# Two query heads turned by one transpose, and low weight parts subtracted on GpSimd, in a hybrid S5 and attention encoder layer

## The chip, the core and the metric

The kernel runs on one core of one Trainium2 chip. The metric is the device time of one execution in microseconds; the time before is a median of 3 runs. The profile comes from one further execution.

## What is computed

The layer works on two sequences of 512 tokens with 1024 features, in fp32. The part that the change touches, cut from the reference:

```
h = rms_norm(x, ln1)
q, k, v, u, g_att, g_ssm = split(h @ w_in)                # 16 query heads, 4 key-value heads of 64
q = rms_norm(q.reshape(b, s, 16, 64), q_gain)             # per head
k = rms_norm(k.reshape(b, s, 4, 64), k_gain)
y_att = windowed_attention(q, k, v, sink, bias, mask)     # blocks of 128 queries, 3 key blocks, a sink per head
y_ssm = s5_branch(u, ...)                                 # y * sigmoid(y @ w_glu + b_glu)
mixed = sigmoid(g_att) * y_att + sigmoid(g_ssm) * y_ssm
x = x + mixed @ w_out
y = x + square(relu(rms_norm(x, ln2) @ w_up)) @ w_down
```

## The kernel before

Each fp32 product is made of three products of reduced-precision operands. An operand is split into a high part (ScalarE copies it to the type fp32r, which rounds it) and a low part (the operand minus the high part); `mm3` multiplies high by high, high by low and low by high. A weight that streams in is thus loaded by SP into a raw tile, copied by ScalarE (L683, L730) and subtracted by VectorE (L684, L731).

The attention stage is a loop of eight passes, one for each key-value head `j` and sequence `sq` (`steps`), and each pass has four steps, one for each block `qb` of 128 queries. The order of the instructions on TensorE, ScalarE, VectorE and GpSimd is the order of the code; SP's order is set by a scheduler. A step interleaves three things:

- The current unit: scores of the four heads (L823), bias and maximum (`largest`, L827), exponentials (L833).
- The unit before: its probabilities are transposed (L839), split into `ph` (ScalarE, L843) and `pl` (VectorE, L848) and multiplied by the values (L855). It has three key blocks when its query block is 1 or 2, so in steps with `qb` 2 and 3, and two otherwise.
- A query tile of the next pass, class `Tile`: 24 matmuls (L772), the square (L778), its sum (L782), the power on GpSimd (L784, L785), the norm `qn` (L789). One step later `turn` transposes the four heads of the tile (L794) into PSUM, `high` (L799) scales them by the gain into rows 0 to 63 of `queries`, `low` (L802) makes the low part in rows 64 to 127. The keys lie in both halves of the rows, so that one score matmul adds the products of both parts.

`pieces_of` gives a pass its weight pieces: the query weights of the next head (`weight_pieces`: four pieces in pass 0, then two in each of passes 1 to 4), and the GLU weights (`glu_pieces`: two pieces in pass 6, four in pass 7). Pass 5 has none. A piece is loaded and copied at the end of a step, and its subtraction is returned as `lower`, which the next step calls behind its third maximum; the last one is called behind the loop. The raw tiles have two buffers (`c_raw`), so a load waits for the subtraction of the piece two before it.

The denominators of the softmax (`Divide`) are inverted and transposed in step 1 of the next pass, written by SP to `rs_scr` (L883), read back spread over the rows as `fac` (L888), and multiplied into the output at the head of step 3 (`multiply`, L893), behind `largest(0)`. GpSimd also issues DMAs: one copy of `y_scr` per step of passes 1 to 4 (L982), and the gates' loads (`load_gates`, L693).

The 128-row tile `gain_q` holds the gain twice, in rows 0 to 63 and in rows 64 to 127.

Of the kernel before, what the change touches and what calls it, by code (L numbers as in the profile page):

```python
# [12 lines left out]
F32 = mybir.dt.float32  # L13
F32R = mybir.dt.float32r
I32 = mybir.dt.int32
AF = mybir.ActivationFunctionType
ALU = mybir.AluOpType
AX = mybir.AxisListType

P = 128  # L20
# [7 lines left out]
CB = 256  # L28
N_HEADS = 16
N_KV = 4  # L30
G = 4
# [32 lines left out]
def hybrid_layer(ctx, tc, x, rel, onehot, w_qkv, w_ug, vectors, lam, coefs, w_glu, w_out, ln2,  # L64
                 w_up, w_down, out):
    nc = tc.nc
    V, S, PE, GP, SP = nc.vector, nc.scalar, nc.tensor, nc.gpsimd, nc.sync
# [36 lines left out]
    ident = const.tile([P, P], F32, name="ident")  # L104
# [5 lines left out]
    bglu_sb, gain_q, gain_k, nsink = [vec[:, a:b] for a, b in ((0, 8), (8, 9), (9, 10), (10, 26))]  # L110
# [561 lines left out]
    wq = wq_cm.__enter__()  # L672
    glu_w, glu_ps, glu_in = {}, {}, {}

    def glu_pieces(m, pool):

        def piece(i):
            if i == 0:
                glu_w[m] = [pool.tile([P, KT, P], F32R, tag=tag, name="g" + tag) for tag in ("c_hi", "c_lo")]
            hi, lo = [q[:, i * KT // 2:(i + 1) * KT // 2, :] for q in glu_w[m]]  # L680
            raw = cpool.tile([P, KT // 2, P], F32, tag="c_raw", name="c_raw")
            SP.dma_start(raw, w_glu[m][:, i * KT // 2:(i + 1) * KT // 2, :])
            S.copy(hi, raw)  # L683
            return lambda: V.tensor_sub(lo, raw, hi.bitcast(F32))  # L684

        return [lambda i=i: piece(i) for i in range(2)]

# [7 lines left out]
    with tc.tile_pool(name="att", bufs=2, reuse_waits="tile") as ap, tc.tile_pool(name="attc", bufs=1, reuse_waits="tile") as ac:  # L695
# [20 lines left out]
        def weight_pieces(j):  # L716

            weights[j] = []
            pool = wq if j % 2 == 0 else cpool

            def piece(i):

                if i % 2 == 0:
                    weights[j].append((pool.tile([P, KT // 2, CB], F32R, tag="c_hi", name="w_hi"),
                                       pool.tile([P, KT // 2, CB], F32R, tag="c_lo", name="w_lo")))
                hi, lo = weights[j][-1]
                sl = slice(i % 2 * 2, i % 2 * 2 + 2)
                raw = cpool.tile([P, 2, CB], F32, tag="c_raw", name="w_raw")
                SP.dma_start(raw, w_qkv[Q_BLK + j][:, i * 2:i * 2 + 2, :])
                S.copy(hi[:, sl, :], raw)  # L730
                return lambda: V.tensor_sub(lo[:, sl, :], raw, hi[:, sl, :].bitcast(F32))  # L731

            return [lambda i=i: piece(i) for i in range(4)]

# [24 lines left out]
        class Tile:  # L759
# [30 lines left out]

            def turn(self):
                self.pt = self.pt or acc()
                for h in range(G):
                    PE.transpose(self.pt[0:64, h * P:(h + 1) * P], self.qn[:, h], ident)  # L794

            def high(self):
                self.ptv = self.pt[0:64].rearrange("p (h t) -> p h t", h=G)
                self.dst = queries[self.key][:, :, self.t * P:(self.t + 1) * P]
                S.activation(self.dst[0:64], self.ptv, AF.Copy, scale=gain_q[0:64])  # L799

            def low(self):
                V.scalar_tensor_tensor(self.dst[64:128], self.ptv, gain_q[0:64], self.dst[0:64].bitcast(F32),  # L802
                                       op0=ALU.mult, op1=ALU.subtract)

        class Unit:

# [151 lines left out]
        def pieces_of(i):  # L958

            if i == 0:  # L960
                return weight_pieces(1)
            if i == 6:
                return glu_pieces(0, wq)
            if i == 7:
                return glu_pieces(1, cpool) + glu_pieces(2, cpool)
            if i % 2 == 1:
                pending[:] = weight_pieces(i // 2 + 2) if i // 2 + 2 < N_KV else []
                return pending[:2]
            return pending[2:]
# [580 lines left out]
```

## Time and profile before

| | us |
|---|---|
| median of 3 runs | 1511.8 (1508.45 to 1513.73) |
| the profiled execution | 1509.57 |
| its span | 1507.8 |
| TensorE matmul, busy | 1452.1 |
| TensorE weight load, busy | 1232.2 |
| VectorE, busy | 1116.3 |
| ScalarE, busy | 763.4 |
| GpSimd, busy | 192.4 |

The attention loop lies between 460 and 695 us of the span. In a row of the timeline the columns are start, duration, engine, line, operation, tiles (out<-in), shapes and count; behind them, in brackets, stands the idle time of the engine and what ended it. In a row of the groups by shape, the figures behind the first bar are the busy time and the mean ns of one instruction, then the idle time ahead of them. In a row of one line's instructions the three durations are minimum, median and maximum in ns. PE is TensorE, PEld its weight loads, DVE VectorE, ACT ScalarE, POOL GpSimd, SP the engine that issues most DMAs (SPq its queue).

### The profile page before, as it was taken

How to read it: one execution, taken by the hardware profiler on the slowest of the kernel's cores; microseconds unless marked ns; L12 is line 12 of the kernel's file. 1: busy time of each engine (PE TensorE's matmuls, PEld its weight loads, DVE VectorE, ACT ScalarE, POOL GpSimd, SP SyncE). 2: the span in 40 equal slices, each digit the busy share in tenths (PEclk: the TensorE clock that was granted, in tenths of full speed). 3: DMA queues.
4: the chain of work that ended last, by engine and by line, in shares of the span. 5: the costliest groups of instructions: out<-in, count | busy, mean ns of one | idle time of the engine just before them, and what ended most of it. 6: DMA issues, size and time to landing. Idle time of an engine off the chain costs nothing. (4 is left out here: it accounts for less than half of the span.)

```text
span 1507.8 us, 22144 instructions
## 1 busy us (share of the span) xinstructions
PE 1452.1 (96%) x8074; PEld 1232.2 (82%) x8074; DVE 1116.3 (74%) x2015; ACT 763.4 (51%) x1362; POOL 192.4 (13%) x362
## 2 busy tenths in 40 slices
PE   6999999999999999997999989999999999999998
PEld 4788888888999998985787878888888888888787
DVE  7998859986647998886985478777777588575653
ACT  6777852235436787783343255544555443433332
POOL 3143341002232332220100000000000000000000
PEclk9999999999999999998999999999999999999999
DMA  4454469239731444373644234444443694454431
GB/s 173 140 168 168 164 211 344 98 111 352 279 103 36 149 138 142 111 257 110 224 164 170 94 103 173 154 153 154 154 154 126 251 361 135 154 181 154 126 122 61
DMA packets 102141, 249.69 MB, mean 166 GB/s; under 512 B 12266, under 2 KB 23786, under 8 KB 102032
## 3 DMA queue, kind: packets, MB, share of 16 engines
q1 hardware_dynamic: 58352, 135.88, 27.6%
q0 software_dynamic: 18048, 57.72, 11.1%
q10 hardware_dynamic: 25632, 54.67, 9.7%
q8 instruction: 64, 1.05, 0.3%
q14 instruction: 45, 0.37, 0.1%
HBM read 173.74 MB, written 90.21 MB: 175 GB/s over the span
## 5 line engine op out<-in xcount | busy, mean ns | idle before, releaser
L185 PE MATMUL acc<-act,c_hi 128*128 128x512 f32 x768 | 249.8, 400 | 1.0 <-DVE act L304 1.0
L117 PE MATMUL bank<-b_lo,a_hi 128*128 128x512 f32 x448 | 174.6, 390 | 1.3 <-DVE b_lo L1419 1.1
L118 PE MATMUL bank<-b_hi,a_lo 128*128 128x512 f32 x448 | 174.3, 389 | 0.0
L116 PE MATMUL bank<-b_hi,a_hi 128*128 128x512 f32 x448 | 173.5, 389 | 0.0
L185 PEld LDWEIGHTS acc<-act,c_hi 128*128 128x128 f32 x768 | 142.2, 189 | 29.2 <-DVE act L304 2.4
L185 PE MATMUL acc<-act,c_lo 128*128 128x512 f32 x384 | 152.5, 397 | 0.0
L1418 ACT CAST a_hi<-d_a 128x1024 fp32r<-128x1024 f32 x56 | 59.1, 1054 | 179.5 <-PE bank L117 176.1
L116 PE MATMUL bank<-act,act 128*128 128x512 f32 x368 | 144.3, 392 | 4.9 <-ACT act L1308 4.9
L117 PE MATMUL bank<-act,act 128*128 128x512 f32 x368 | 144.0, 391 | 0.0
L118 PE MATMUL bank<-act,act 128*128 128x512 f32 x368 | 143.9, 391 | 0.0
L1419 DVE TENSOR_TENSOR a_lo<-d_a,a_hi 128x1024 fp32r<-128x1024 f32 x56 | 68.5, 1223 | 100.0 <-ACT a_hi L1418 100.0
L772 PE MATMUL acc<-w_hi,act 128*128 128x256 f32 x512 | 116.1, 295 | 0.0
L117 PEld LDWEIGHTS bank<-b_lo,a_hi 128*128 128x128 f32 x448 | 84.1, 188 | 19.6 <-DVE b_lo L1419 2.3
L116 PEld LDWEIGHTS bank<-b_hi,a_hi 128*128 128x128 f32 x448 | 84.1, 188 | 17.6
L118 PEld LDWEIGHTS bank<-b_hi,a_lo 128*128 128x128 f32 x448 | 84.1, 188 | 17.4
L123 PE MATMUL acc<-act,gc_hi 128*128 128x512 f32 x256 | 83.9, 407 | 13.7 <-ACT ga L1133 10.7
L772 PEld LDWEIGHTS acc<-w_hi,act 128*128 128x128 f32 x512 | 86.9, 189 | 3.7
L116 PEld LDWEIGHTS bank<-act,act 128*128 128x128 f32 x368 | 69.6, 189 | 19.8 <-ACT act L1308 5.3
L185 PEld LDWEIGHTS acc<-act,c_lo 128*128 128x128 f32 x384 | 72.6, 189 | 13.8 <-DVE c_lo L176 0.5
L833 ACT ACTIVATE p<-p,nmx 128x257 f32<-128x257 f32 (+1 forms) x128 | 72.2, 564 | 22.7 <-DVE nmx L827 21.1
L118 PEld LDWEIGHTS bank<-act,act 128*128 128x128 f32 x368 | 69.6, 189 | 14.8 <-DVE act L1309 0.4
L117 PEld LDWEIGHTS bank<-act,act 128*128 128x128 f32 x368 | 69.6, 189 | 14.4
(328 smaller groups left out, 3426.5 us busy)
## 6 DMA issues: line engine op xcount, KB each, us to landing
d_a<-a_scr SPq DMA_DIRECT2D x56, 512.0 KB, 3.6
u_raw<-in_w_up_dram SPq DMA_DIRECT2D x32, 512.0 KB, 5.1
a_scr<-t ACTq DMA_DIRECT2D x64, 256.0 KB, 5.0
k<-in_w_down_dram SPq DMA_DIRECT2D x32, 512.0 KB, 6.0
c_raw<-in_w_ug_dram SPq DMA_DIRECT2D x48, 256.0 KB, 3.8
a_scr<-a ACTq DMA_DIRECT2D x46, 256.0 KB, 2.1
ct_scr<-ctab POOLq DMA_DIRECT2D x16, 576.0 KB, 3.9
ctab_in<-ct_scr POOLq DMA_DIRECT2D x16, 576.0 KB, 7.8
```

The source lines that it names most:

```text
L116: PE.matmul(ps, a[0], b[0], start=first, stop=False)
L117: PE.matmul(ps, a[0], b[1], start=False, stop=False)
L118: PE.matmul(ps, a[1], b[0], start=False, stop=last)
L123: PE.matmul(ps, w[wi][:, k, :], rows[yi], start=k + p == 0, stop=k == KT - 1 and p == 2)
L185: PE.matmul(ps, w[wi][:, k, :], hT[s][hi][:, k, :], start=n == 0, stop=n == 3 * KT - 1)
L772: PE.matmul(self.ps, hT[sq][act][:, k, col:col + P], w[:, k % 4, :], start=i == 0, stop=i == 3 * KT - 1)
L833: S.activation(p, p, AF.Exp, bias=self.nmx[:, h:h + 1], scale=-1.0, accum_out=self.sums[:, h, self.qb:self.qb + 1])
L1418: S.copy(hi, src)
L1419: V.tensor_sub(lo, src, hi.bitcast(F32))
```

## The change

`turn` transposes two heads at once: the 128 columns of two neighbouring heads become 128 rows of PSUM, so a tile takes two transposes in place of four. The even heads then lie in rows 0 to 63 and the odd ones in rows 64 to 127. `high` and `low` become two instructions each, one for the even and one for the odd heads, on 64 rows by 256 columns in place of 64 by 512. For odd heads the high part stands in rows 64 to 127 of `queries` and the low part in rows 0 to 63.

The subtraction of the query weight pieces, and of the GLU pieces that are taken inside the loop, moves from VectorE to GpSimd (18 subtractions). The GLU pieces behind the loop stay on VectorE.

```diff
-    def glu_pieces(m, pool):
+    def glu_pieces(m, pool, eng=V):
...
-            return lambda: V.tensor_sub(lo, raw, hi.bitcast(F32))
+            return lambda: eng.tensor_tensor(lo, raw, hi.bitcast(F32), op=ALU.subtract)
...
-                return lambda: V.tensor_sub(lo[:, sl, :], raw, hi[:, sl, :].bitcast(F32))
+                return lambda: GP.tensor_tensor(lo[:, sl, :], raw, hi[:, sl, :].bitcast(F32), op=ALU.subtract)
...
             def turn(self):
                 self.pt = self.pt or acc()
-                for h in range(G):
-                    PE.transpose(self.pt[0:64, h * P:(h + 1) * P], self.qn[:, h], ident)
+                for m in range(2):
+                    PE.transpose(self.pt[:, m * P:(m + 1) * P],
+                                 self.qn[:, 2 * m:2 * m + 2].rearrange("p e d -> p (e d)"), ident)
 
             def high(self):
-                self.ptv = self.pt[0:64].rearrange("p (h t) -> p h t", h=G)
-                self.dst = queries[self.key][:, :, self.t * P:(self.t + 1) * P]
-                S.activation(self.dst[0:64], self.ptv, AF.Copy, scale=gain_q[0:64])
+                self.ptv = self.pt[:, 0:CB].rearrange("p (m t) -> p m t", m=2)
+                self.dst = [queries[self.key][:, e::2, self.t * P:(self.t + 1) * P] for e in range(2)]
+                for dst, rows in zip(self.dst, (slice(0, 64), slice(64, 128))):
+                    S.activation(dst[rows], self.ptv[rows], AF.Copy, scale=gain_q[rows])
 
             def low(self):
-                V.scalar_tensor_tensor(self.dst[64:128], self.ptv, gain_q[0:64], self.dst[0:64].bitcast(F32),
-                                       op0=ALU.mult, op1=ALU.subtract)
+                for dst, rows, other in zip(self.dst, (slice(0, 64), slice(64, 128)), (slice(64, 128), slice(0, 64))):
+                    V.scalar_tensor_tensor(dst[other], self.ptv[rows], gain_q[rows], dst[rows].bitcast(F32),
+                                           op0=ALU.mult, op1=ALU.subtract)
...
-                return glu_pieces(0, wq)
+                return glu_pieces(0, wq, GP)
...
-                return glu_pieces(1, cpool) + glu_pieces(2, cpool)
+                return glu_pieces(1, cpool, GP) + glu_pieces(2, cpool, GP)
```

Three places show how the instructions move. The lines of the changed kernel are 3 higher from here on (L805 is `low`, L830 the maximum, L851 the low part of the probabilities, L818 the copy of the sink). On VectorE, in step 1 of pass 2, from the reciprocal of the denominators to the low part of the queries, before:

```order
L875 RECIPROCAL rsum<-sm 128x16
L827 ISA p,nmx<-sps,bias,vec 128x384
L827 ISA nmx 128x1
L731 TENSOR_TENSOR w_lo<-w_raw,w_hi 128x512
L848 TENSOR_TENSOR pl<-tps,ph 128x512
L827 ISA p,nmx<-sps,bias,vec 128x384
L827 ISA nmx 128x1
L802 SCALAR_TENSOR_TENSOR qa<-acc,vec,qa 64x4x128
```

The same stretch of the changed kernel:

```order
L878 RECIPROCAL rsum<-sm 128x16
L830 ISA p,nmx<-sps,bias,vec 128x384
L830 ISA nmx 128x1
L851 TENSOR_TENSOR pl<-tps,ph 128x512
L830 ISA p,nmx<-sps,bias,vec 128x384
L830 ISA nmx 128x1
L805 SCALAR_TENSOR_TENSOR qa<-acc,vec,qa 64x2x128 x2
```

The subtraction is gone from between the maximum and the low part of the probabilities, and the low part of the queries is two instructions. On GpSimd, in step 1 of pass 3, from its power to the copies for the step behind it, before:

```order
L784 TENSOR_SCALAR ms<-ms 128x4
L785 TENSOR_TENSOR rq<-ms,neg_half 128x4
L982 DMA y_scr<-y_scr 16x64x128
L815 COPY p<-vec 128x4
L784 TENSOR_SCALAR ms<-ms 128x4
```

And of the changed kernel:

```order
L784 TENSOR_SCALAR ms<-ms 128x4
L785 TENSOR_TENSOR rq<-ms,neg_half 128x4
L731 TENSOR_TENSOR w_lo<-w_raw,w_hi 128x512
L985 DMA y_scr<-y_scr 16x64x128
L818 COPY p<-vec 128x4
```

The subtraction now stands behind the power of its step and ahead of the next step's DRAM copy and sink copy. On SP's queue, in pass 7, from the denominators' store to the next GLU load, before:

```order
L883 DMA rs_scr<-row 16x128
L682 DMA c_raw<-in_w_glu_dram 128x512
L888 DMA fac<-rs_scr 64x2x512 x2
L682 DMA c_raw<-in_w_glu_dram 128x512
L894 DMA mix_scr<-ya 128x2x512
L1102 DMA w_raw<-in_w_out_dram 128x512
```

And of the changed kernel:

```order
L886 DMA rs_scr<-row 16x128
L682 DMA c_raw<-in_w_glu_dram 128x512 x2
L891 DMA fac<-rs_scr 64x2x512 x2
L1105 DMA w_raw<-in_w_out_dram 128x512
L897 DMA mix_scr<-ya 128x2x512
```

The second GLU load, which waits for the subtraction of the piece two before it, has moved ahead of the read of the denominators. In passes 1 to 4 the order on SP is as it was, with a weight load ahead of the store of the denominators. On GpSimd the last subtraction, which was on VectorE, now stands ahead of the gate loads that follow the loop.

## The prediction

> **What bounds the kernel now.** I read the page, the waits of the attention loop, its steps one by one in the timeline, and the groups by shape. A pass is one key-value head of one sequence (eight, numbered 0 to 7); a step is one query block of a pass, so 5.2 is the third block of pass 5.
>
> ```profile
> PE 1452.1 (96%) x8074; PEld 1232.2 (82%) x8074; DVE 1116.3 (74%) x2015; ACT 763.4 (51%) x1362; POOL 192.4 (13%) x362
> 486.78 0.28 PE L823 MATMUL sps<-kh,qa 128*128 128x256 f32 x1
> 515.92 0.28 PE L823 MATMUL sps<-kh,qa 128*128 128x256 f32 x1
> 545.38 0.28 PE L823 MATMUL sps<-kh,qa 128*128 128x256 f32 x1
> 574.46 0.28 PE L823 MATMUL sps<-kh,qa 128*128 128x256 f32 x1
> 604.33 0.28 PE L823 MATMUL sps<-kh,qa 128*128 128x256 f32 x1
> 632.92 0.28 PE L823 MATMUL sps<-kh,qa 128*128 128x256 f32 x1
> 662.02 0.28 PE L823 MATMUL sps<-kh,qa 128*128 128x256 f32 x1
> ```
>
> The first row says that TensorE is nearly always busy, but it counts a matmul until its modelled end. The other rows are the first score matmul of passes 1 to 7, so their differences are the lengths of passes 1 to 6: 29.14, 29.46, 29.08, 29.87, 28.60 and 29.10 us. All six do the same arithmetic on TensorE. Pass 5 alone subtracts no weights; the others have two subtractions on VectorE. The trace thus holds its own experiment, and a pass with subtractions costs at least 0.48 us more. Where it costs that is seen in block 2 of passes 3 and 5:
>
> ```profile
> 560.04 1.04 POOL L785 TENSOR_TENSOR rq<-ms,neg_half 128x4 f32<-128x4 f32 x1
> 562.67 0.60 PE L794 MATMUL acc<-ident,qn 128*64 128x128 f32 x4
> 562.97 0.68 DVE L731 TENSOR_TENSOR w_lo<-w_raw,w_hi 128x512 fp32r<-128x512 f32 x1
> 563.10 0.60 PE L839 MATMUL tps<-ident,p 128*128 128x128 f32 x4
> 563.57 0.68 DVE L848 TENSOR_TENSOR pl<-tps,ph 128x512 fp32r<-128x512 f32 x1
> 566.34 0.19 PEld L855 LDWEIGHTS po<-pl,va 128*128 128x128 f32 x1 [0.83 <-DVE pl L848]
> 622.58 0.67 ACT L799 ACTIVATE qa<-acc,vec 64x512 fp32r<-64x512 f32 x1
> 623.28 0.75 DVE L802 SCALAR_TENSOR_TENSOR qa<-acc,vec,qa 64x512 fp32r<-64x512 f32 x1 [0.21 <-ACT qa L799]
> 624.80 0.19 PEld L855 LDWEIGHTS po<-pl,va 128*128 128x128 f32 x1 [0.38 <-DVE pl L848]
> ```
>
> The subtraction L731 keeps VectorE for 0.60 us (562.97 to 563.57), between two steps of the softmax. At the block's end TensorE waits for the last low part of the probabilities, 0.83 us in 3.2 and 0.38 in 5.2: 0.45 more. So blocks 2 and 3, where the unit before has three key blocks, are paced by VectorE, and even without a subtraction VectorE waits there 0.21 us for ScalarE's high part of the queries (L799). In these blocks TensorE has time to spare. A second wait stands at the head of block 3, where the softmax denominators come back from memory:
>
> ```profile
> DVE ya L893 <- DMA fac<-rs_scr: 0.9, 2, 0.7
> 557.11 0.33 SPq L729 DMA_DIRECT2D w_raw<-in_w_qkv_dram  x1
> 557.53 0.38 SPq L883 DMA_DIRECT2D rs_scr<-row  x1
> 560.84 1.23 SPq L888 DMA_DIRECT2D fac<-rs_scr  x2
> 616.33 0.32 SPq L883 DMA_DIRECT2D rs_scr<-row  x1
> 617.73 1.23 SPq L888 DMA_DIRECT2D fac<-rs_scr  x2
> fac<-rs_scr SPq DMA_DIRECT2D x16, 256.0 KB, 4.1
> ```
>
> Twice the multiply L893 waits for that DMA, 0.9 us together, and passes 2 and 4 are the long ones. L888 can't be issued before L883 has landed: 3.3 us in pass 3, where a weight load was issued just ahead on the same queue, 1.4 us in pass 5, where none was.
>
> **The change part by part.** *Two transposes fewer per query tile.* Four start at 562.67 and the next at 563.10, 0.108 us each; the full-width ones behind them last the same 0.60 for four, so two fewer save 0.22 us of TensorE. Three of the 32 tiles lie before the loop:
>
> ```profile
> 434.00:459.70 25.70, 25.70 (x218) 25.70 (x217) 6.89 (x14) 4.38 (x10) 4.27 (x7) 1.00 0.01 1
> ```
>
> TensorE is full there and VectorE a quarter busy: 3 x 0.22 = 0.65 us gained. In the loop only blocks 0 and 1 can use it, where the next item takes most of it.
>
> *High and low parts in two halves.* Their prices are not in the trace, but the same kinds of work at 512 and 256 columns are:
>
> ```profile
> L802 DVE SCALAR_TENSOR_TENSOR qa<-acc,vec,qa 64x512 fp32r<-64x512 f32 x29 | 21.6, 744 | 3.2 <-ACT qa L799 2.5
> L799 ACT ACTIVATE qa<-acc,vec 64x512 fp32r<-64x512 f32 x29 | 19.5, 672 | 0.7 <-PE acc L794 0.5
> L848 DVE TENSOR_TENSOR pl<-tps,ph 128x512 fp32r<-128x512 f32 x78 | 53.5, 686 | 0.4
> L789 DVE TENSOR_TENSOR qn<-acc,rq 128x256 f32<-128x256 f32 x28 | 11.6, 413 | 0.0
> L843 ACT CAST ph<-tps 128x512 fp32r<-128x512 f32 x78 | 44.9, 576 | 5.4 <-PE tps L839 4.8
> L778 ACT ACTIVATE sq<-acc 128x256 f32<-128x256 f32 x28 | 10.6, 380 | 6.4 <-PE acc L772 5.7
> ```
>
> VectorE takes 273 ns less for 256 columns, ScalarE 196. So I take a half at 744 - 273 = 471 and 672 - 196 = 476 ns (bounds: half price, 372 and 336; full price, 744 and 672). VectorE then works 0.20 us longer per tile, ScalarE 0.28. In blocks 2 and 3 this is hidden: the first low half needs the first high half only, so it starts 0.20 us earlier than 623.28, which fills the 0.21 of waiting, and two halves end at about 624.03, when the one ended. At half price the block gains 0.2, at full price it loses 0.6. In blocks 0 and 1 TensorE's 2 x 0.22 shrinks to about 0.15, because the longer VectorE and ScalarE work takes the slack there. I give back 0.1 for blocks 2 and 3, where ScalarE's next high part moves back by up to 0.28. Net gain: 0.05 us per pass (bounds: 0.45 gained, 0.7 lost).
>
> *Subtractions moved from VectorE to GpSimd* (12 for query weights, 6 for GLU weights).
>
> ```profile
> L745 POOL COPY kd<-kn 128x512 f32<-128x512 f32 x8 | 4.8, 606 | 0.0
> L785 POOL TENSOR_TENSOR rq<-ms,neg_half x32: 1037/1041/1049, 428.9 to 662.8; 128x4 f32<-128x4 f32 x32
> L815 POOL COPY p<-vec x32: 182/203/472, 420.9 to 670.9; 128x4 f32<-128x4 f32 x32
> ```
>
> GpSimd copies a tile of this size in 0.61 us; reading two tiles, I take twice that, 1.2 (bounds 0.61 and 2.7). By the Trainium skill (GPSIMD Engine Reference, § Performance versus the Vector engine) an add of two inputs takes it 4497 ns at 2048 elements, so about 1.1 here as an estimate. On POOL the subtraction stands behind the power of its block, which ends at 561.08, and so would end at 562.3, 1.3 us before VectorE's did; behind it are, in passes 1 to 4, a DRAM copy and a 0.2 us copy for the next block, which have time to spare. Passes with subtractions become like pass 5, less 0.05: 28.55. From their lengths that is 0.59 + 0.91 + 0.53 + 1.32 + 0.05 + 0.55 = 3.95 us for passes 1 to 6. This holds the 0.9 of DMA waits: the weight load ahead of L883 waits for the subtraction of the step, so it goes out 1.3 us earlier, and the denominators land earlier by about that (bounds 0 and 1.9, the 3.3 us trip against the 1.4). Without this the shorter block 2 only lengthens the wait. Pass 0 has three of its subtractions inside, with no multiply: 0.55 (bounds 0 and 0.9). Pass 7 has one query tile: 0.2 gained (bounds 0 and 0.22); its subtractions hide, as its projections are over.
>
> *What the order costs at the end.*
>
> ```profile
> 674.80 0.62 ACT L683 CAST gc_hi<-c_raw 128x512 fp32r<-128x512 f32 x1
> 675.44 1.64 SPq L888 DMA_DIRECT2D fac<-rs_scr  x2
> 681.84 1.22 DVE L893 TENSOR_TENSOR ya<-ya,fac 128x1024 f32<-128x1024 f32 x1
> 687.86 0.61 POOL L693 DMA_DIRECT2D ga<-ga_scr  x1 [16.76 <-PE acc L123]
> 688.76 0.62 ACT L683 CAST gc_hi<-c_raw 128x512 fp32r<-128x512 f32 x1
> 702.10 1.23 DVE L893 TENSOR_TENSOR ya<-ya,fac 128x1024 f32<-128x1024 f32 x1 [6.95 <-DMA fac<-rs_scr]
> ```
>
> In pass 7 SP now has a second GLU load ahead of L888. It waits for a subtraction, whose high part ends at 675.42; with 1.2 for GpSimd and 0.3 for the issue, L888 goes out at 677.0 instead of 675.44. At 4.1 us from issue to landing the last part came at 681.2 at the latest (677.08 + 4.1), 0.6 or more ahead of the multiply at 681.84; it now comes 1.6 later. I take 0.8 lost (bounds 0 and 1.6). At the end the gate loads (L693), issued at 687.86, now stand behind the last subtraction (689.4 + 1.2 = 690.6). They then run beside the last trip of the denominators, for which VectorE waits 6.95 us: 0.5 lost (bounds 0 and 1.9, the two trips above).
>
> *Sum:* 0.65 + 0.55 + 3.95 + 0.2 - 0.8 - 0.5 = 4.05 us less. The profiled execution took 1509.57 (span 1507.8 and 1.8 around it), so 1505.5; the median shown is 1511.8, 2.2 above it, so the median becomes 1507.7.
>
> **The rivals.** *GpSimd holds up VectorE (slower).* If VectorE stands still while GpSimd subtracts, each of the seven subtractions on VectorE's path (block 2 of passes 0 to 4 and 6, block 3 of pass 0) costs 1.2 instead of 0.60: the 0.45 gained on each (3.15) becomes 0.6 lost (4.2). The six in blocks 1, cheap today, would push 0 to 0.6 each onto the path; I take 0.3 (1.8). That is 4.05 - 3.15 - 4.2 - 1.8, so 5.1 us slower, 1516.9. The path's seven alone decide from a hold of 0.73 us on (0.60 + 0.9 / 7). For it: one of 32 small POOL copies took 472 ns against a median of 203, so POOL at least can be held. Against it: all 32 powers took 1037 to 1049 ns, whatever VectorE did. The Trainium skill (Perfetto Trace Analysis, § Optimizing Scalar/DVE Operations) warns that moving work between these two might not help, as they share a read port. By SBUF — State Buffer, § Who interferes with whom, only VectorE instructions with two SBUF inputs, or in a two-port mode, are held, and in the loop that is the multiply and hardly more.
>
> *The denominators still arrive late (no change).* If their landing hangs on other traffic, or GpSimd takes 2.7 us so that the weight load goes no earlier, passes 2 to 4 keep their waits and also lose block 2's 0.45: 0.9 + 3 x 0.45 = 2.25 lost, 1.8 faster, 1510.0. For it: pass 5, with the short trip, also has no DRAM copies from POOL beside it. Against it: it has no load ahead either, and the load is the one on the same queue; the rows can't tell the two apart.
>
> *TensorE bounds the loop after all (much faster).* Then all 29 tiles that are turned inside the loop give their 0.22, 6.4 instead of the 0.55 counted (7 x 0.05 and 0.2): 9.9 faster, 1501.9. For it: 96% busy. Against it: the waits for `pl`. The Trainium skill (Perfetto Trace Analysis, its opening note) calls matmul busy time a bad metric, as matmuls are pipelined; the waits agree.
>
> **How the numbers follow.** Chances: forecast 0.60, late denominators 0.20, held VectorE 0.12, TensorE bound 0.08. A measurement of this kernel tells 0.3% (4.5 us) from no change, and the forecast of 4.05 lies just inside it. With its bounds (pass 0, the splits, the two late costs: about 2 us either way) it gives 0.28 faster, 0.30 within, 0.02 slower; late denominators 0.01, 0.18, 0.01; held VectorE 0, 0.04, 0.08; TensorE 0.08 faster. Together 0.37, 0.52 and 0.11. The range leaves out most of the TensorE case and of the held one: 1503.0 to 1513.0.
>
> **What would show it.** Right: 18 POOL rows of about 1.2 us; L855's wait for `pl` at 0.4 in all blocks 2; passes 1 to 6 at 28.5; L893 without a wait in passes 2 and 4, and with one of about 0.8 in pass 7; L802's halves near 0.47. Wrong: passes that stay at 29 with VectorE rows longer or gaps behind GpSimd; L893 waiting in passes 1 to 4; passes near 27.7, with TensorE never waiting.

## The result and the profile after

The changed kernel takes 1517.0 us (median of 10 runs, 1514.62 to 1519.97), the kernel before 1510.6 beside it (10 runs, 1508.45 to 1513.73): a ratio of 1.0042, with a 95% interval of 1.0033 to 1.0051. It is 6.4 us slower, where 4.1 faster was forecast. The span of the profiled execution grew from 1507.8 to 1515.4 us. Single executions of e1, e8 and e15 below, and one of the kernel before, ran 8 to 193% longer as a whole; the medians and ratios leave them out, and as in e1 and e8 it was the profiled one, those two profiles are not read.

The timeline of the changed kernel gives the starts of passes 1 to 7 by their first score matmul:

```profile
486.75 0.28 PE L826 MATMUL sps<-kh,qa 128*128 128x256 f32 x1
518.73 0.28 PE L826 MATMUL sps<-kh,qa 128*128 128x256 f32 x1
548.84 0.28 PE L826 MATMUL sps<-kh,qa 128*128 128x256 f32 x1
578.92 0.28 PE L826 MATMUL sps<-kh,qa 128*128 128x256 f32 x1
609.03 0.28 PE L826 MATMUL sps<-kh,qa 128*128 128x256 f32 x1
639.15 0.28 PE L826 MATMUL sps<-kh,qa 128*128 128x256 f32 x1
669.24 0.27 PE L826 MATMUL sps<-kh,qa 128*128 128x256 f32 x1
```

Passes 1 to 6 take 31.98, 30.11, 30.08, 30.11, 30.12 and 30.09 us, 182.5 in all where they took 175.2. Pass 5, which subtracts nothing in either kernel, went from 28.60 to 30.12: the loss cannot be GpSimd's alone. The rest is small. The stretch of the first query tiles, from the first L772 to the loop, fell from 38.46 to 37.80; pass 0 grew from 27.02 to 27.62; from the start of pass 7 to the end it grew from 845.77 to 846.13.

By blocks, 5.0 to 5.3 took 6.50, 6.60, 7.72 and 7.78 us and now take 6.28, 6.70, 8.85 and 8.29. (Pass 1 is longer than the others because its multiply waits 1.81 us for the denominators.) What happens at the end of 5.2 is seen in its timeline:

```profile
627.79 0.94 ACT L801 ACTIVATE qa<-acc,vec 64x256 fp32r<-64x256 f32 x2
628.19 0.08 DVE L830 DVE_READ_ACCUMULATOR2_ANT nmx<- 128x1 f32 x1
628.76 0.98 DVE L805 SCALAR_TENSOR_TENSOR qa<-acc,vec,qa 64x256 fp32r<-64x256 f32 x2 [0.49 <-ACT qa L801]
629.77 0.69 DVE L851 TENSOR_TENSOR pl<-tps,ph 128x512 fp32r<-128x512 f32 x1
630.52 0.19 PEld L858 LDWEIGHTS po<-pl,va 128*128 128x128 f32 x1 [0.94 <-DVE pl L851]
```

VectorE has its fourth maximum at 628.27. The first high half is done 0.45 us after 627.79, at 628.24. Still VectorE stands for 0.49 us, until both high halves are done at 628.73, and only then begins the first low half. The two low halves then hold it until 629.77, 1.01 us, where the one low part held it 0.78 (623.28 to 624.06). From the start of the high part to the start of `pl` it is 1.98 us instead of 1.48, and TensorE waits for that `pl` 0.94 instead of 0.38.

That is 0.5 of the 1.13 us by which block 5.2 grew. The rest stands at its start, where VectorE still has the tile of block 5.1 to finish. Before, where 5.2 starts at 617.42:

```profile
616.92 0.74 DVE L802 SCALAR_TENSOR_TENSOR qa<-acc,vec,qa 64x512 fp32r<-64x512 f32 x1 [0.37 <-ACT qa L799]
618.43 0.61 DVE L827 CUSTOM_DVE_ANT_0 p<-sps,bias,vec 128x384 f32<-128x384 f32 x1
```

And in the changed kernel, where it starts at 622.01:

```profile
622.03 0.98 DVE L805 SCALAR_TENSOR_TENSOR qa<-acc,vec,qa 64x256 fp32r<-64x256 f32 x2 [0.64 <-ACT qa L801]
623.62 0.62 DVE L830 CUSTOM_DVE_ANT_0 p<-sps,bias,vec 128x384 f32<-128x384 f32 x1
```

The low part of the tile of 5.1 held VectorE until 0.24 us into the block, and the two halves hold it until 1.00. The block's first maximum starts 1.61 us into it in place of 1.01.

In the whole loop TensorE's waits for `pl` grew, as the two lists of waits show, before and after (us in total, times, longest):

```profile
PEld po L855 <- DVE pl L848: 9.2, 22, 0.8
```

```profile
PEld po L858 <- DVE pl L851: 15.1, 22, 0.9
```

The groups of the changed kernel show that each instruction has the size that was forecast:

```profile
L805 DVE SCALAR_TENSOR_TENSOR qa<-acc,vec,qa 64x256 fp32r<-64x256 f32 x58 | 28.0, 484 | 13.1 <-ACT qa L801 12.1
L801 ACT ACTIVATE qa<-acc,vec 64x256 fp32r<-64x256 f32 x58 | 26.9, 464 | 0.5
L731 POOL TENSOR_TENSOR w_lo<-w_raw,w_hi 128x512 fp32r<-128x512 f32 x12 | 15.5, 1289 | 0.0
```

484 and 464 ns for the halves, 1289 for GpSimd's subtraction. What was not forecast is the 12.1 us for which VectorE waits for ScalarE's high halves (2.5 for the high part before).

### The profile page after: what moved, and what is told of

Read it like the earlier page. It is cut to its first block, busy times and chain, and to the rows that moved or that the text cites. A ratio compares the mean times of both kernels' runs of the same rounds, so it can differ in the third digit from the quotient of the medians.

```text
span 1515.4 us, 22090 instructions
## 1 busy us (share of the span) xinstructions
PE 1450.6 (96%) x8010; PEld 1226.8 (81%) x8010; DVE 1113.8 (74%) x2029; ACT 774.0 (51%) x1394; POOL 217.4 (14%) x380
## 4 chain that ended last, share of the span: by engine, by line
PE 76%; DVE 8%; issue 5%; ACT 5%; DMA 4%; POOL 1%; SPq 0%; ACTq 0%; DVEq 0%; POOLq 0%
PE acc L185 13%; PE bank L117 13%; PE bank L118 13%; PE bank L116 13%; PE acc L123 5%; PE acc L772 3%; PE acc L117 2%; PE acc L118 2%; PE acc L116 2%; PE sps L547 2%; PE sps L826 2%; PE po L858 2%; DVE pl L851 1%; PE tps L842 1%; PE acc L225 1%
## 5 line engine op out<-in xcount | busy, mean ns | idle before, releaser
L772 PE MATMUL acc<-w_hi,act 128*128 128x256 f32 x512 | 116.1, 295 | 0.0
L772 PEld LDWEIGHTS acc<-w_hi,act 128*128 128x128 f32 x512 | 87.0, 189 | 3.6
```

Source lines behind the costliest of these rows:

```text
L772: PE.matmul(self.ps, hT[sq][act][:, k, col:col + P], w[:, k % 4, :], start=i == 0, stop=i == 3 * KT - 1)
```

## The experiments

The theory after this profile, W: the loss is in the halves. The first low half waits for both high halves, and what stands behind it, `pl` above all, comes late. The first rival, G: the move to GpSimd costs it. All times are compared with the kernel before in the same series (medians 1508.8 to 1510.6). "Pass" is the length of pass 5 unless another is named.

| | median us | ratio, 95% interval | pass |
|---|---|---|---|
| changed kernel | 1517.0 | 1.0042 (1.0033 to 1.0051) | 30.12 |
| e1, e6: GpSimd alone | 1508.2, 1508.0 | 0.9993 (0.9983 to 1.0003), 0.9986 (0.9976 to 0.9995) | 28.63 |
| e2: two transposes and halves alone | 1517.3 | 1.0056 (1.0039 to 1.0072) | 30.10 |
| e3: halves on the same rows, one tile | 1511.9 | 1.0022 (1.0009 to 1.0035) | 29.15 |
| e4: the same, two tiles | 1516.6 | 1.0055 (1.0036 to 1.0074) | 30.25 |
| e5: even and odd heads side by side | 1517.0 | 1.0052 (1.0036 to 1.0067) | 30.09 |
| e14: e3 with alternating rows | 1515.7 | 1.0043 (1.0030 to 1.0055) | 29.87 |
| e7: changed kernel, high halves ahead | 1527.1 | 1.0122 (1.0105 to 1.0138) | 31.40 |
| e8: e6, high part ahead | 1526.9 | 1.0119 (1.0104 to 1.0135) | not read |
| e9: changed kernel, `pl` ahead of the halves | 1509.2 | 1.0002 (0.9992 to 1.0011) | 28.73 |
| e10: e6, `pl` ahead of the low part | 1505.3 | 0.9978 (0.9963 to 0.9993) | 28.10 |
| e11: e6, DRAM copies elsewhere | 1507.3 | 0.9988 (0.9978 to 0.9999) | 28.61 |
| e12: e10 with e11, multiply behind the additions | 1504.3 | 0.9965 (0.9950 to 0.9980) | 28.17 |
| e13: e12 with two transposes and halves | 1507.6 | 0.9991 (0.9981 to 1.0002) | 28.72 |
| e15: e12 with the multiply on GpSimd | 1499.9 | 0.9938 (0.9922 to 0.9955) | 27.50 |

e6 repeats e1 for its profile.

**e1, e6 and e2: which half of the change costs it.** e1 and e6 are the kernel before with the edit for GpSimd alone, all 18 subtractions (cut):

```diff
-                return lambda: V.tensor_sub(lo[:, sl, :], raw, hi[:, sl, :].bitcast(F32))
+                return lambda: GP.tensor_tensor(lo[:, sl, :], raw, hi[:, sl, :].bitcast(F32), op=ALU.subtract)
...
-                return glu_pieces(0, wq)
+                return glu_pieces(0, wq, GP)
```

> The kernel before, with only the 18 subtractions moved to GpSimd; transposes, high and low as before. Theory W (the loss lies in the two low halves: the first one waits until the second high half is done, 0.49 us per query tile): no such wait exists here, so passes 1 to 6 are all near pass 5 of before, 28.6 us, and the whole takes 1507 to 1509 us. Rival G (GpSimd's subtractions, or the SP and POOL order that they set, cause the loss): passes near 30 us and 1513 us or more.

> The kernel of e1_gp_alone once more, for its profile. If the forecast for GpSimd's part is right in its place and e1's small gain comes from one late DMA: passes 1 to 6 at 28.6 us but for one or two, in which the multiply waits for the denominators 0.5 to 2 us, as in pass 1 of the changed kernel; blocks 2 all at 7.7 us. If the subtractions on GpSimd cost the loop something everywhere: blocks 2 above 7.9 us in all passes. The whole 1507 to 1509 us.

e2 is the changed kernel with these lines taken back.

> The changed kernel with all subtractions back on VectorE; two transposes and the halves stay. Theory W: VectorE waits about 0.49 us for the second high half in each block without a subtraction in it; where a subtraction stands ahead, it covers that wait. Passes 1 to 6 near 30 us, the whole 1515 to 1518 us. Rival G: passes no longer than before (28.6 to 29.9 us), 1510 us or less.

The starts of passes 2, 3, 5 and 6 of e6, and its longest wait for the denominators:

```profile
516.75 0.28 PE L823 MATMUL sps<-kh,qa 128*128 128x256 f32 x1
546.52 0.28 PE L823 MATMUL sps<-kh,qa 128*128 128x256 f32 x1
...
603.70 0.28 PE L823 MATMUL sps<-kh,qa 128*128 128x256 f32 x1
632.33 0.28 PE L823 MATMUL sps<-kh,qa 128*128 128x256 f32 x1
...
539.58 1.23 DVE L893 TENSOR_TENSOR ya<-ya,fac 128x1024 f32<-128x1024 f32 x1 [1.08 <-DMA fac<-rs_scr]
```

All blocks 2 of e6 take 7.72 us, with a subtraction or without, and passes 3 to 6 28.57 to 28.63. So GpSimd holds nobody, and this half of the change does what the forecast said, but for pass 2 (29.77), where the multiply waits 1.08 us. G falls: e6 is faster, e2 is as slow as the changed kernel. In e2 passes 1 to 4 and 6 take 30.25 to 30.27 us and pass 5, without subtractions, 30.10. Here the subtractions on VectorE are nearly free: block 1 takes 7.00 us with one and 6.69 in pass 5 without, block 2 8.69 with one and 8.84 without. They fill the time in which VectorE would stand for the high halves, 0.48 us in 5.2 and nothing in 3.2. So the two edits do not add up, as the forecast's sum had them do: with the halves in place, the move to GpSimd is worth 0.15 us a pass, and pass 1 pays more than that back, as its multiply waits 1.81 us in the changed kernel and in e2 not at all.

**e3, e4, e5, e14: why the halves cost so much.** The program itself shows the wait. ScalarE raises its semaphore (the counter by which one engine waits for another) once, behind both high halves. With their waits, the two low halves of a tile of the changed kernel stand in the program as:

```
L805 SCALAR_TENSOR_TENSOR qa<-acc,vec,qa 64x2x128 [waits PE_49,Activation_49]
L805 SCALAR_TENSOR_TENSOR qa<-acc,vec,qa 64x2x128
```

In e4, where each half has a PSUM tile of its own, ScalarE raises it behind each high half, and they read:

```
L805 SCALAR_TENSOR_TENSOR qa<-acc,vec,qa 64x2x128 [waits Activation_49]
L805 SCALAR_TENSOR_TENSOR qa<-tps,vec,qa 64x2x128 [waits Activation_49]
```

e3 and e4 split the high and low part of e6 by neighbouring heads, all on the old rows:

```diff
-                S.activation(self.dst[0:64], self.ptv, AF.Copy, scale=gain_q[0:64])
+                self.halves = [(dst[:, 2 * m:2 * m + 2], ptv[:, 2 * m:2 * m + 2]) for m in range(2)]
+                for dst, ptv in self.halves:
+                    S.activation(dst[0:64], ptv, AF.Copy, scale=gain_q[0:64])
```

> As e1_gp_alone, but high and low split into halves of two neighbouring heads each (64 rows by 256 columns, rows 0 to 63 as before, next to each other in memory), all four transposes in one PSUM tile. Theory W (the wait comes with two engines reading one PSUM tile, not with rows or columns): the first low half starts only after the second high half, passes 1 to 6 near 30.3 us, 1517 to 1520 us. Rival R (the odd heads' rows 64 to 127, or every second head's columns, cause the wait): no wait, passes 28.6 to 28.9 us, 1507 to 1511 us.

In e4 the second pair of heads is transposed into a tile of `tps()`.

> As e3_split_one_tile, but the second pair of heads is transposed into a PSUM tile of its own, so that a low half shares its tile with its own high half alone. Theory W: the first low half starts right behind the first high half, passes 1 to 6 at 28.6 to 28.9 us, 1507 to 1511 us. Rival H (two halves of 0.46 to 0.48 us are simply more work than one of 0.67 to 0.74, wait or no wait): passes stay near 30 us, as in e3.

Block 5.2 of e3:

```profile
621.77 0.81 ACT L801 ACTIVATE qa<-acc,vec 64x256 fp32r<-64x256 f32 x2
622.62 0.87 DVE L805 SCALAR_TENSOR_TENSOR qa<-acc,vec,qa 64x256 fp32r<-64x256 f32 x2 [0.36 <-ACT qa L801]
623.51 0.69 DVE L851 TENSOR_TENSOR pl<-tps,ph 128x512 fp32r<-128x512 f32 x1
```

And of e4:

```profile
628.69 0.45 ACT L801 ACTIVATE qa<-acc,vec 64x256 fp32r<-64x256 f32 x1
628.70 0.66 PE L842 MATMUL tps<-ident,p 128*128 128x128 f32 x4 [0.40 <-DVE pl L851]
629.21 0.48 DVE L805 SCALAR_TENSOR_TENSOR qa<-acc,vec,qa 64x256 fp32r<-64x256 f32 x1
630.11 0.69 DVE L851 TENSOR_TENSOR pl<-tps,ph 128x512 fp32r<-128x512 f32 x1
```

e4 confirms the mechanism. The first low half now starts 0.52 us after the first high half, where it was 0.85 in e3 and 0.97 in the changed kernel, and `pl` starts 1.42 us after it (e3 1.74). Its time is a miss: it takes one more of the two `tps` buffers per step, and TensorE's transposes now wait for one until a `pl` is done (0.40 us in the second row), so the price of the wait can't be read from it. e3 waits, as W says, but passes take 29.15 us and not 30.3. So W is only part of it. In e3 the two high halves together last 0.81 us and in the changed kernel 0.94, the low ones 0.87 and 0.98: on the same rows the second begins before the first has ended. The new theory, N: instructions whose rows start elsewhere than those of the one ahead do not overlap with it. e5 tells it from the step over every second head:

```diff
-                self.dst = [queries[self.key][:, e::2, self.t * P:(self.t + 1) * P] for e in range(2)]
+                self.dst = [queries[self.key][:, 2 * e:2 * e + 2, self.t * P:(self.t + 1) * P] for e in range(2)]
...
-                qs = queries[self.j, self.sq][:, h, self.qb * P:(self.qb + 1) * P]
+                qs = queries[self.j, self.sq][:, h % 2 * 2 + h // 2, self.qb * P:(self.qb + 1) * P]
```

> The changed kernel, with the even heads kept in slots 0 and 1 of the query tile and the odd ones in slots 2 and 3, so that each half writes one piece of columns and not every second head. Theory N (two neighbouring instructions on different row ranges, 0 to 63 and 64 to 127, do not overlap: in the changed kernel the second high half starts 0.47 us after the first and the second low half 0.49 after the first, where in e3, on the same rows, these are 0.36 and 0.40): nothing changes, passes 1 to 6 at 30.1 us, 1516 to 1518 us. Rival C (the step over every second head does it, or holds the first low half back): 0.36 and 0.40, passes near 29 us, 1511 us or less.

Nothing changed, as N says: pass 30.09, and the second halves start 0.47 and 0.49 us after the first. e14 is e3 with the second pair's high part in rows 64 to 127 and its low part in rows 0 to 63:

```diff
-                self.halves = [(dst[:, 2 * m:2 * m + 2], ptv[:, 2 * m:2 * m + 2]) for m in range(2)]
+                halves = (slice(0, 64), slice(64, 128))
+                self.halves = [(rows, dst[rows, 2 * m:2 * m + 2], dst[other, 2 * m:2 * m + 2], ptv[:, 2 * m:2 * m + 2])
+                               for m, (rows, other) in enumerate((halves, halves[::-1]))]
```

> As e3_split_one_tile (four transposes, two halves out of rows 0 to 63 of one PSUM tile), but the second pair of heads has its high part in rows 64 to 127 of the query tile and its low part in rows 0 to 63, as the odd heads have in the changed kernel. Nothing else differs from e3. Theory N (an instruction whose rows start elsewhere than those of the one ahead does not overlap with it): the second high half starts 0.47 us after the first in place of 0.36, the second low half 0.49 in place of 0.40, and passes 1 to 6 are near 30.0 to 30.3 us in place of 29.15, the whole 1515 to 1518 us. Rival P (what separates e3 from the changed kernel is the two transposes, or reading PSUM rows 64 to 127): 0.36 and 0.40 as in e3, passes near 29.15 us, 1511 to 1513 us.

```profile
626.72 0.94 ACT L803 ACTIVATE qa<-acc,vec 64x256 fp32r<-64x256 f32 x2
627.69 0.97 DVE L807 SCALAR_TENSOR_TENSOR qa<-acc,vec,qa 64x256 fp32r<-64x256 f32 x2 [0.48 <-ACT qa L803]
628.69 0.69 DVE L852 TENSOR_TENSOR pl<-tps,ph 128x512 fp32r<-128x512 f32 x1
```

The rows alone bring the two pairs to 0.94 and 0.97 us and the pass from 29.15 to 29.87, a little less than N's 30.0. The Trainium skill (VectorE: DVE Perf Modes, § Two Vector instructions with no wait between them) states it as a rule: a VectorE instruction is held until all earlier ones have finished if its input starts in another group of 32 rows than the last read from the same memory, or its output in another than the last write. e3 and e14 agree: 0.40 and 0.49 us from the first low half to the second. The trace of before could have told it. Its two additions per step write rows 0 to 63 and then 64 to 127, and the norm is an instruction of the same length on all rows:

```profile
618.97 0.84 DVE L865 TENSOR_TENSOR ya<-po,ol 64x256 f32<-64x256 f32 x2
619.84 0.62 DVE L827 CUSTOM_DVE_ANT_0 p<-sps,bias,vec 128x384 f32<-128x384 f32 x1
...
620.99 0.42 DVE L789 TENSOR_TENSOR qn<-acc,rq 128x256 f32<-128x256 f32 x1
621.32 0.61 DVE L827 CUSTOM_DVE_ANT_0 p<-sps,bias,vec 128x384 f32<-128x384 f32 x1
```

Two additions keep VectorE for 0.87 us, 0.43 each. The norm keeps it for 0.33, though it lasts 0.42 as well.

So the 1.5 us of a pass from e6 (28.63) to the changed kernel (30.12) are: 0.5 for two halves in one PSUM tile on the same rows (e3), 0.7 for the alternating rows (e14), and 0.25 that came with the two transposes and PSUM rows 64 to 127, which no run separates (block 0 is 0.22 shorter than in e14, block 2 0.48 longer, as its first maximum starts 1.61 us into it in place of 1.17). The Trainium skill (PSUM — Partial Sum Buffer, § PSUM bank collisions raise a hardware error) states that two engines may use one bank at a time if they are in different groups of 32 rows. By that rule the first low half of the changed kernel (rows 0 to 63) would not have to wait for the second high half (rows 64 to 127). No run here shows it; a kernel without that wait wasn't tried, since the order of two engines on one PSUM tile is made when the program is built.

**e7 and e8: the high part earlier.** If the wait for the high halves is what costs, having them ready earlier should help:

```diff
                         prev.high(1)
                     project(4)
+                    if rows:
+                        rows.turn()
+                        rows.high()
...
-                    if rows:
-                        rows.turn()
...
                     if rows:
-                        rows.high()
                         rows.low()
```

> The changed kernel, with the two transposes and both high halves moved ahead of the third exponential, so that the high parts are ready before VectorE's fourth maximum ends. Theory W: VectorE no longer waits 0.49 us ahead of the first low half; blocks 2 and 3 get shorter by about 0.5 us each, passes 1 to 6 near 28.9 to 29.2 us, 1509 to 1512 us. Rival A (ScalarE itself is the bound there, so that its two halves delay the third exponential instead): passes stay near 30 us, 1515 us or more.

> The kernel of e1_gp_alone (four transposes, one high and one low part), with transposes and high part moved ahead in the same way. Theory W: the waits of 0.21 and 0.24 us for the high part in blocks 2 and 3 go, passes near 28.2 us, 1504 to 1507 us. Rival A: 1508 us or more, passes at 28.6 us or longer.

Both are misses, and slower by 10 us and more than the kernels that they were made of. The group of the transposes in e7:

```profile
L794 PE MATMUL acc<-ident,qn 128*128 128x128 f32 x56 | 12.0, 296 | 23.7 <-DVE qn L789 23.7
```

VectorE's waits ahead of the low halves fell from 13.1 to 1.2 us, as the theory has it, but the place was wrong: TensorE now stands 23.7 us for the norm that VectorE has yet to make. So it was not ScalarE that bounds, as rival A had it. For e8 no profile shows the cause; the same wait is likely.

**e9 and e10: `pl` first.** The other way is to take the halves off the path: the third `turn`, `high` and `low` of the probabilities go ahead of the query tile's.

```diff
-                    if rows:
-                        rows.turn()
                     if n3 > 2:
                         prev.turn(2)
+                    if rows:
+                        rows.turn()
...
+                    if n3 > 2:
+                        prev.high(2)
+                        prev.low(2)
                     if rows:
                         rows.high()
                         rows.low()
-                    if n3 > 2:
-                        prev.high(2)
...
-                    if n3 > 2:
-                        prev.low(2)
```

> The changed kernel, with the third high and low part of the probabilities put ahead of the query tile's high and low halves in blocks 2 and 3 (on TensorE their transposes first, on ScalarE ph first, on VectorE pl first). Theory W: what the changed kernel loses is that pl, for which TensorE waits at the end of these blocks, stands behind the wait for both high halves and behind the two low halves. With pl ahead of them the wait of 0.49 us and the longer halves only use up VectorE's slack, and blocks 2 and 3 fall from 8.85 and 8.29 to 7.1 to 7.7 us; passes 27.3 to 28.5 us, the whole 1499 to 1507 us. Rival A (VectorE or ScalarE are full in these blocks, wherever the halves stand): blocks 2 and 3 stay within 0.2 us of 8.85 and 8.29, 1514 us or more.

> The kernel of e6_gp_alone_again (four transposes, one high and one low part) with the same order as in e9. Theory W: the waits of 0.22 and 0.24 us for the high part go from the path, blocks 2 and 3 fall from 7.72 and 7.79 to 7.1 to 7.4 us, passes 27.3 to 28.0 us, 1499 to 1504 us. Compared with e9 it tells what the two transposes are worth once the halves are off the path: e9 should then be faster by up to 0.22 us in blocks 0 to 3. Rival A: 1507 to 1509 us, as e6.

The start of pass 5 in e9, TensorE's longest wait in its last block, and the start of pass 6:

```profile
601.18 0.28 PE L826 MATMUL sps<-kh,qa 128*128 128x256 f32 x1
625.52 0.47 PE L858 MATMUL po<-ph,va 128*128 128x512 f32 x1 [0.59 <-DVE ya L868]
629.91 0.28 PE L826 MATMUL sps<-kh,qa 128*128 128x256 f32 x1
```

The order alone brings the changed kernel from 1.0042 to 1.0002 of before, about 6 us, and its passes from 30.1 to 28.7 us (but for pass 1, 30.89). e6 gains 0.5 us a pass by the same order, as e10 shows, so the halves cost 0.6 us a pass in the new order (28.10 to 28.73) where they cost 1.5 in the old one: more than half of the loss was their place ahead of `pl`. The size was over-forecast: block 2 came to 7.74 us and block 3 to 8.03, and TensorE's next wait shows in the middle row, for VectorE's additions. e10 gets blocks 2 and 3 to 7.41 and 7.62 us, passes 1 and 4 to 6 to 28.10 to 28.15. But its pass 2 takes 31.25, as the multiply waits there 1.79 us for its DMA and more waits follow. And e10 is faster than e9, not slower: two transposes fewer do not pay for the halves that come with them.

**e11: who makes the denominators late.** In passes 1 to 4 GpSimd issues a DRAM copy in each block; e11 moves them.

```diff
-                    if 1 <= i < 5:
-                        e, t = divmod((i - 1) * NB + qb, T)
...
+                    for n in {0: (0, 1), 3: (2, 3)}.get(qb, ()) if 1 <= i < 5 else ():
+                        e, t = divmod((i - 1) * NB + n, T)
```

> The kernel of e6_gp_alone_again, with the four DRAM copies that GpSimd issues in each of passes 1 to 4 moved from one per block to two in block 0 and two in block 3, so that none starts while the denominators are on their way (blocks 1 and 2). If those copies make the denominators late (the forecast's second rival): the multiply waits in no pass, pass 2 falls from 29.8 to 28.6 us, the trips of rs_scr and fac are below 3.5 and 4.5 us in passes 1 to 4, the whole 1506 to 1507.5 us. If the weight load ahead on SP's queue makes them late: trips stay at 3.8 to 4.3 and 5 to 6 us, one or two multiplies still wait.

The DMA issues around the late denominators in pass 1 of the changed kernel:

```profile
497.01 0.82 POOL L985 DMA_DIRECT2D y_scr<-y_scr  x1
497.09 0.33 SPq L729 DMA_DIRECT2D w_raw<-in_w_qkv_dram  x1
498.87 0.34 SPq L886 DMA_DIRECT2D rs_scr<-row  x1
504.16 1.34 SPq L891 DMA_DIRECT2D fac<-rs_scr  x2
511.29 1.23 DVE L896 TENSOR_TENSOR ya<-ya,fac 128x1024 f32<-128x1024 f32 x1 [1.81 <-DMA fac<-rs_scr]
```

And in pass 1 of e11:

```profile
498.05 0.33 SPq L729 DMA_DIRECT2D w_raw<-in_w_qkv_dram  x1
499.71 0.34 SPq L883 DMA_DIRECT2D rs_scr<-row  x1
501.28 1.35 SPq L888 DMA_DIRECT2D fac<-rs_scr  x2
```

In the changed kernel the copy stands behind the subtraction on GpSimd, and the load waits for that same subtraction, so both start at 497.0. The 8 KB of denominators behind them take 5.3 us to land (498.87 to 504.14), and `fac` another 6. In e11 the load stands ahead of them just as well, 1.66 us, and without a copy they land in 1.55 us (1.35 to 2.29 in passes 1 to 4, where e6 has 3.5 to 4.2). No multiply of passes 1 to 6 waits, and all take 28.58 to 28.66 us. So it is the copy and not the load. The gain is what e6's pass 2 had lost, 1.2 us of the trace; the ratios to the kernel before (0.9986 and 0.9988) don't show it, as it lies inside the intervals.

**e12, e13 and e15: the best version, and what two transposes are worth in it.** e12 joins e10 and e11 and puts `late.multiply()` behind `owed.add()`. e13 is the same with two transposes and halves.

> The kernel of e10_gp_tile_last (four transposes, one high and one low part, pl ahead of them), with the copies apart as in e11 and the multiply by the denominators put behind the two additions of the unit before (in e9 and e10 TensorE waits 0.56 to 0.87 us in block 3 for those additions, which stand behind the multiply of 1.22 us). Expected: no multiply waits for its DMA, block 3 falls from 7.62 to 7.0 to 7.3 us, passes 27.4 to 27.9 us, the whole 1498 to 1502 us.

> The same kernel as e12 with two transposes and the halves. Theory W and N (wait for both high halves, no overlap of the halves): they still cost VectorE 0.24 and ScalarE 0.37 us a tile, so blocks 1 and 2 stay longer than in e12 (6.68 against 6.60, 7.7 against 7.4 us), and only blocks 0 and the prelude gain 0.22 us each; passes 0.1 to 0.4 us longer than e12's, the whole 0 to 3 us slower than e12. Rival T (once the halves are off the path, the two transposes fewer pay 0.22 us in every block): 5 us faster than e12.

Pass 5 of e12, by its start and the next one's:

```profile
598.79 0.28 PE L823 MATMUL sps<-kh,qa 128*128 128x256 f32 x1
626.96 0.28 PE L823 MATMUL sps<-kh,qa 128*128 128x256 f32 x1
```

And of e13:

```profile
598.66 0.28 PE L826 MATMUL sps<-kh,qa 128*128 128x256 f32 x1
627.38 0.28 PE L826 MATMUL sps<-kh,qa 128*128 128x256 f32 x1
```

28.17 and 28.72: with all else equal the new transposes with their halves cost 0.55 us a pass and the kernel 3.3 us in the median (the two profiled executions alone, at 1504.6 and 1504.2 us, would not show it). They are worth 0.2 us in blocks 0 (6.49 to 6.29) and 0.65 ahead of the loop, and cost 0.03, 0.33 and 0.40 in blocks 1, 2 and 3. Rival T falls. What e12 missed is block 3, 7.63 us as in e10: the additions come earlier, and in 5.3 TensorE waits for the maximum behind the multiply (0.23 us) and for `pl` (0.31) instead. VectorE is full there: it stands idle once, for 0.34 us at the block's start. e15 takes the multiply off it (cut):

```diff
-                        late.multiply()
+                        late.multiply(GP)
```

> The kernel of e12, with the multiply by the denominators moved to GpSimd inside the loop (the last one stays on VectorE). VectorE then has 1.14 us less to do in block 3, where it is full: block 3 falls from 7.62 to 6.9 to 7.3 us, passes 27.4 to 27.9 us, the whole 1500 to 1503 us. If GpSimd's multiply (about 2.6 us, twice the subtraction of half the size) holds VectorE up or delays the next block's work on GpSimd, block 3 or block 0 gets longer: 1505 us or more.

```profile
595.48 0.28 PE L823 MATMUL sps<-kh,qa 128*128 128x256 f32 x1
622.98 0.28 PE L823 MATMUL sps<-kh,qa 128*128 128x256 f32 x1
L893 POOL TENSOR_TENSOR ya<-ya,fac 128x1024 f32<-128x1024 f32 x7 | 16.7, 2392 | 8.1 <-DMA fac<-rs_scr 8.1
```

Block 3 falls to 6.97 us and the pass to 27.50 (pass 2 takes 28.36, as VectorE waits there 1.96 us for the load of a bias tile). The multiply takes GpSimd 2.39 us where VectorE took 1.22, and nobody waits for it. With 1499.9 us, a ratio of 0.9938 (0.9922 to 0.9955), e15 beats both kernels. It has the GpSimd half of the change and not the transposes.

## Why the prediction was wrong, point by point

- **What bounds the kernel:** right. Blocks 2 and 3 are paced by VectorE, TensorE has time to spare there, and passes with less work for VectorE are the short ones (e6, e15).
- **Two transposes fewer:** right in size ahead of the loop, 0.66 us (38.46 to 37.80) for the 0.65 forecast.
- **High and low in two halves:** the step that failed. The prices of one half (471 and 476 ns forecast, 484 and 464 measured) were right. The sentence "the first low half needs the first high half only, so it starts 0.20 us earlier than 623.28" was wrong: the program has it wait for both, since both engines read one PSUM tile, and it starts 0.97 us after the first high half begins, not right at that half's end, after 0.48. And two instructions were priced by how long one lasts, not by when the next one can start. On VectorE that cost little (from the start of the low part to `pl` 0.78 us became 1.01, 0.23 more for 0.20 forecast); on ScalarE 0.57 us became 0.96, 0.39 more for 0.28, as instructions on the same rows overlap and the halves, on alternating rows, do not. The forecast "two halves end at about 624.03, when the one ended" thus missed 0.5 us in block 3 and 1.13 in block 2: 0.5 for its own tile and 0.6 for the tile of block 1, whose halves reach into it. The forecast had no term for that carry, and it costs more than the 0.2 that block 0 saves. A net gain of 0.05 us a pass was forecast, with 0.7 lost as the bound; 1.5 were lost, outside the bounds.
- **Subtractions on GpSimd:** right by itself. They take 1.29 us (1.2 forecast), blocks 2 with them are as long as without (7.72), and pass 0, passes 1 to 6 and the end together gain 0.50 + 2.33 + 0.10 = 2.93 us in e6. The forecast had 0.55 + 3.65 - 1.3 = 2.9 for the same work. That the sums agree is luck: two errors cancel, those of the next two points. The medians of e1 and e6 gain less, 1.1 and 2.1 us. The change as a whole could not show it, as the sum took the two edits for independent.
- **Denominators in time:** half right. The multiplies of passes 2 and 4 wait no more in the changed kernel, but not for the reason given. The weight load does go out earlier (1.8 us ahead of the denominators in place of 0.4), yet they take 3.8 to 5.3 us to land in passes 1 to 4, not less than before (3.1 to 4.3); the longer blocks 2 only give them time, and pass 1 waits 1.81 us. The rival "late denominators" named the DRAM copies as its evidence, and e11 shows that it was right in that.
- **What the order costs at the end:** the multiply of pass 7 does not wait, if barely (`fac` lands at 688.85, it starts at 688.87), so the 0.8 us did not come. The last store of the denominators does run beside the gate loads, 1.98 us in place of 1.35. From the start of pass 7 on the changed kernel lost 0.36 us, where 1.1 were forecast (0.2 gained, 0.8 and 0.5 lost); e6 lost nothing there. Between the traces of all kernels here this stretch lies between 845.1 and 849.2 us, so that 0.36 says little.
- **The rivals:** "GpSimd holds up VectorE" gave 1516.9 us, next to what was measured, for a reason that e6 excludes. A right number from a wrong mechanism. Of VectorE's instructions only the multiply was seen longer beside a subtraction on GpSimd, as the prediction had said of it: in pass 7 of e12 and e13, where the subtraction had begun 0.34 us earlier, it took 2.03 us in place of 1.22. In pass 7 of the changed kernel it began 0.49 us ahead of the subtraction, which then took 1.88 us in place of 1.29. "TensorE bounds the loop" fell with e13: two transposes fewer, with their halves, make the loop longer even where `pl` goes ahead of the halves. A rival in which the halves themselves are late was missing, though the change rewrites them.

## What to carry to other kernels

Splitting one instruction into two lets the second engine start early only if the first piece is released by itself: look in the built program at which instruction raises the semaphore, above all where two engines read one PSUM tile. Follow the late engine into the next block too, as what it still has to do there counts again. Price an instruction by the distance to the next start on its engine, taken from a pair on the same rows in the one case and on changing rows in the other, and not by its duration. Before fewer instructions on the busiest engine are bought with more on the one that paces the block, see which of the two is waited for; here the order of `pl` and the halves was worth more to the changed kernel (about 6 us) than either edit.

## What the runs showed of the hardware

- Halves on the same rows start 0.36 us (ScalarE) and 0.40 us (VectorE) after each other though they last 0.46 and 0.47 (e3); on alternating rows 0.47 and 0.49 (e14). ScalarE behaves like VectorE in this.
- An 8 KB store to memory took 1.34 us to land in pass 5 with nothing beside it, 1.35 to 2.29 us with a 256 KB load begun 1.66 us ahead on its queue (passes 1 to 4 of e11), and 3.8 to 5.3 us with that load and a 512 KB copy begun 1.8 us ahead (passes 1 to 4 of the changed kernel).
- A multiply of two 128x1024 tiles took GpSimd 2.39 us and VectorE 1.22, and a subtraction of 128x512 1.29 and 0.68. VectorE's other instructions took no longer beside the subtraction (block 2 of e6 7.72 us with it and without). Where multiply and subtraction met, the one that began second took longer (the multiply 2.03 us in e12, the subtraction 1.88 in the changed kernel).
